# Scattering the experts' results to token order instead of gathering them

## The chip, the cores and the metric

The kernel runs on 1 core of one Trainium2 chip. The metric is the device time of one execution in microseconds (us), as the median of several runs. A profiled execution of the kernel before is there beside the times; PE is TensorE, DVE is VectorE, ACT is ScalarE, POOL is GpSimd and SP is SyncE.

## The reference

Two transformer blocks over 1024 tokens of 1024 channels, in f32. Each block ends in a mixture of experts: every token chooses two experts (16 experts in the first block, 32 in the second), each expert is a gated two-layer network with 256 hidden channels, and the two results of a token are added with their weights. Cut to what matters here:

```
# first block; the second is alike with 32 experts
for e in range(N_EXPERTS):
    he = silu(t @ exp_w1[e]) * (t @ exp_w3[e])
    y = y + comb[:, e:e + 1] * (he @ exp_w2[e])      # comb is zero but for two experts of a token
h = h + y
```

## The kernel before

Attention and the other mixers come first in each block, then the router (`route`), then the experts (`moe`), then a part that adds the results to the stream: `join` behind the first block's experts (it also starts the second block), and the loop at the end of `run` behind the second block's.

**Places.** Each expert has a place, a fixed number of rows: nine of 192 and seven of 128 in the first block (2624 rows), and 128, 128, 128, 192, three more of 128, four of 96, six of 80, ten of 64 and five of 48 in the second (2704 rows). A place of 192 is worked as two units, 128 and 64 rows. There are 1024 x 2 = 2048 choices, so many rows are empty. What does not fit goes to a loop over blocks of 128 rows, `moe_rest`, whose trip count is read from the router's result.

**Experts.** `moe` walks the places in a fixed order. In iteration i, POOL issues an indirect gather of the tokens of the place after next (`gather`, L1702, from the DRAM tensor `vs` by the table `idx`), PE turns the tokens of the next place (`xT`, L1726 or L1715), works `up` of this place (L1748), then `down` of the place before (L200). ACT (and DVE) evacuate that result to a tile y, and POOL writes y to rows of the DRAM tensor `ys` (L1801). So POOL's queue, which is worked in order, holds: gather of place i+2, half of a weight's split (L176), the one or two puts of place i-1, gather of place i+3, and so on. SP issues all weight loads, eight pieces ahead; six pieces make an expert.

**Reading back.** `fetch` gathers, for a tile of 128 tokens, the rows of their first and of their second choice by the table `slot`: two indirect DMAs of 512 KB on POOL (L1894). `join` fetches three tiles ahead. The last loop of `run` fetches six tiles ahead, adds them (L1903) and stores each tile on SP (L2711).

**Zeros.** Rows past the fixed places are written by the loop alone and may never be written, so `make_ys` fills them with zeros: 40 DMAs of 512 KB on SP from a tile that DVE clears (L840, L846), issued while the first block's branches are merged.

Storage is a ring of 42 tiles of 128 x 1056 f32 (`t()`), worked through in program order. Each engine and each queue waits in order; the waits come from the program's tiles and tensors, by the range that an instruction names.

Of the kernel before, what the change touches and what calls it, by code (L numbers as in the profile page):

```python
# [9 lines left out]
F32 = mybir.dt.float32  # L10
# [9 lines left out]
T = 1024  # L20
D = 1024
# [17 lines left out]
class Side:  # L39
    """Work that fills in between the blocks of a main stream, in its own order."""  # L40
# [20 lines left out]
    # a block of the main stream of this length has been put in  # L61
# [31 lines left out]
    # the most blocks that any counts (2 * T in all, the places past NP in falling order) leave to the loop  # L93
# [21 lines left out]
class Kern:  # L115
# [87 lines left out]
    def consts(self):  # L203
# [24 lines left out]
        gp.iota(self.tid, pattern=[[0, 2], [1, 8]], base=0, channel_multiplier=0,  # L228
# [4 lines left out]
        # ones under the high and the low part of each head's row  # L233
# [27 lines left out]
    # 1/sqrt(ss/n + eps), some columns at a time, with one step of Newton's after the table's root  # L261
# [23 lines left out]
    # transpose four token tiles (already scaled), gains on the way, hi and lo  # L285
# [10 lines left out]
    # out^T tile = w^T u^T, three passes, with the columns ahead of the tokens or without  # L296
# [26 lines left out]
    # ======================================================= attention  # L323
    # maxima of half of one head's queries from a first product, fed back as a row
    def attn_max(self, H, half):
# [3 lines left out]
        for ii in range(4):  # L329
# [7 lines left out]
            for j, (c0, c1, s0) in enumerate(ch):  # L337
# [30 lines left out]
    # halves of heads one after the other; the product with v follows LAG blocks behind  # L368
# [60 lines left out]
    # two heads to one tile of channels: unnormalized values and the sums  # L429
# [5 lines left out]
    # halves of pairs of heads one after the other; the products with v follow LAG blocks behind,  # L435
    # those of the two heads next to each other in the array, and so do the sums of the rows
# [78 lines left out]
    # sums of the rows of both heads and halves, each on a quarter of the partitions  # L515
# [9 lines left out]
    # what is left of a pair once its last product is in, with the delays in blocks  # L525
# [16 lines left out]
    # ======================================================= block one  # L542
# [39 lines left out]
    # rows and their norm, channel major; v of the tokens that are ready between the steps  # L582
# [89 lines left out]
    # v with a column of ones for each head, 128 keys to a block, and the forget gates  # L672
# [49 lines left out]
        # to rows [head, token], running sum, negated, as hi and lo  # L722
# [18 lines left out]
    # l = log(1 + w) for w >= 0  # L741
# [13 lines left out]
    # channel-major k and q of two heads  # L755
# [11 lines left out]
    # two sets of operands of the product of q and k, with their constant rows  # L767
# [6 lines left out]
    # rows of sums and partial maxima, filled once where nothing is written later  # L774
# [13 lines left out]
    # 1 / sums: the four rows go over all partitions and back  # L788
# [47 lines left out]
    # rows of the experts' results; those that only the loop may write start as zeros  # L836
    def make_ys(self):
        self.ys = {}
        z = self.t()
        self.ve.memset(z, 0.0)  # L840
        for lay in self.lays:
            ys = self.ys[lay.E] = self.d([lay.RB + lay.MS * 128, D], F32, f"ys{lay.E}")
            for b in range(lay.MS):
                if b % 3 == 0:
                    yield
                self.sy.dma_start(ys[lay.RB + b * 128:lay.RB + (b + 1) * 128, :], z[:, :D])  # L846
# [76 lines left out]
    def pair_units(self, pairs, prep, Hs, done):  # L923
# [5 lines left out]
        # what waits for another engine is put off behind the next steps  # L929
# [48 lines left out]
    # inputs of the convolution and of the pool, channel major, with the keys ahead of the tokens  # L978
# [35 lines left out]
    def conv_one(self):  # L1014
# [13 lines left out]
        # layer norm over the 256 channels, then silu  # L1028
# [78 lines left out]
    def merge_one(self):  # L1107
# [27 lines left out]
        zero = self.make_ys()  # L1135
        for m in range(8):
            next(zero, None)
            next(zero, None)
            g = gate()
            mt = self.t()  # L1140
            branch(self.w(), 0, self.ych, 4, g, True, mt)
            self.gp.dma_start(mc[m], mt[:, :T])
        self.ych = None
        for _ in zero:
            pass
# [28 lines left out]
    # ======================================================= output product, norm, router  # L1174
    # the router's weights ahead of their use
# [10 lines left out]
    # merged channels of half of the tokens, two to a tile  # L1186
# [13 lines left out]
    def mix_out(self, resid, g_ffn, lay, tag):  # L1200
# [9 lines left out]
        # high and low parts of the merged channels  # L1210
# [6 lines left out]
        # on the rows before their norm, with its gains in the weights  # L1217
        # some rows at a time, in three steps
# [31 lines left out]
        # a step of the product for rows i  # L1250
# [38 lines left out]
        def evac(i, p0, p1):  # L1289
# [16 lines left out]
            # columns stored as (k p) with d = p * 8 + k  # L1306
# [68 lines left out]
    # ======================================================= routing  # L1375
    # experts of each token, tiles t0 to t1: one-hot rows of both choices and their running sums
    def choose(self, L, lay, t0, t1, R):
# [24 lines left out]
        # one-hot of the first place that holds the maximum  # L1402
# [29 lines left out]
        # rank of each choice within its expert  # L1432
# [3 lines left out]
        # tokens by expert and rank, by one-hot products  # L1436
# [9 lines left out]
        for k in range(2):  # L1446
            ve.tensor_tensor(C2[:, k, :, 1, :], R["A"][:, k, ts, :], bc(self.tid[:, ts], E), op=OP.mult)
# [8 lines left out]
    def route_new(self, lay):  # L1456
# [15 lines left out]
        # on partitions: the experts twice, the second time with a weight of 128  # L1472
# [7 lines left out]
        # the experts' numbers under their counts, the fixed ones ahead, as a row and as a column  # L1480
# [16 lines left out]
    def route(self, L, lay, R, tag):  # L1497
# [8 lines left out]
        # places of the experts  # L1506
# [13 lines left out]
        te.matmul(ps[:1, 2 * E:3 * E], R["ec"][:E2], perm, start=True, stop=True)  # L1520
        idx = sm.tile([128, 3, E], I32, name="idx", tag="idx", bufs=1)
        ve.tensor_copy(idx[:, 0, :], ps[:, 0:E])
        ve.tensor_copy(idx[0:1, 2, :], ps[0:1, 2 * E:3 * E])
        ve.tensor_copy(idx[:W - 128, 1, :], ps[:W - 128, E:2 * E])
        r = dict(lay=lay, idx=idx)
# [4 lines left out]
    # slots of the choices and their weights, and the loop's blocks  # L1530
    def route_rest(self, L, lay, R, tag, r, tr, ar, bt):
# [63 lines left out]
        slot = sm.tile([128, 16], I32, name="slot", tag="slot", bufs=1)  # L1595
        ve.tensor_copy(slot, sl)
# [3 lines left out]
        # tokens of the loop's blocks  # L1600
# [1143 lines left out]
```

## Time and profile before

| | us |
|---|---|
| median of 3 runs | 2699.92 |
| lowest and highest run | 2695.99, 2700.57 |
| span of the profiled execution | 2697.9 |
| PE busy | 2482.7 (92%) |
| POOL busy | 665.8 (25%) |

The span runs from the first to the last instruction of one profiled execution, whose own time is not given apart from it; the median of the runs is 2.0 us above it. The first block's experts run from about 899 to 1135 us of the span, `join` from about 1143 us, the second block's experts from about 2293 to 2651 us, and the last loop behind them.

### The profile page before, as it was taken

The page shows a single profiled execution, that of the slowest core. Times are in us where ns is not written, and L with a number is a line of the kernel's source. Part 1 is how long each engine was busy: PE and PEld are TensorE (multiplying, and loading weights), DVE is VectorE, ACT ScalarE, POOL GpSimd, SP SyncE. Part 2 cuts the span into 40 slices and gives each one's busy share as a digit, 9 for nine tenths or more (in the row PEclk, how much of TensorE's full clock was granted, in tenths as well). Part 3 has the DMA queues.
Part 4 walks back from the last instruction along what each step waited for, and adds up shares of the span by engine and source line. Part 5 has one row for each costly group of instructions (what it writes and reads, how often), then busy time and mean ns, then how long its engine had stood idle before and what let it go on. Part 6 is the DMA issues. An engine that isn't in the chain of part 4 may idle for free. (4 is left out here: it accounts for less than half of the span.)

```text
span 2697.9 us, 35605 instructions
## 1 busy us (share of the span) xinstructions
PE 2482.7 (92%) x12353; PEld 1919.6 (71%) x12353; DVE 1651.6 (61%) x2653; ACT 1235.6 (46%) x2169; POOL 665.8 (25%) x698
## 2 busy tenths in 40 slices
PE   7999999999999799769999999989999998898992
PEld 7975696778877577668788888986555576665551
DVE  4235339742345798674665463567777465898884
ACT  4236521231132567665334333436555532677771
POOL 1011111000001234450000002244455511343343
PEclk9999999999999899989999999999999999899996
DMA  4000245522252699762222120334222254699996
GB/s 135 25 9 10 62 137 195 199 89 88 94 181 80 205 305 340 246 196 71 63 86 61 57 77 20 112 122 139 75 84 90 92 196 156 214 357 356 353 356 237
DMA packets 251766, 402.78 MB, mean 149 GB/s; under 512 B 31280, under 2 KB 142160, under 8 KB 251584
## 3 DMA queue, kind: packets, MB, share of 16 engines
q1 hardware_dynamic: 221616, 300.25, 34.3%
q0 software_dynamic: 29968, 100.22, 10.7%
q8 instruction: 99, 1.62, 0.2%
q14 instruction: 83, 0.68, 0.1%
HBM read 304.71 MB, written 95.29 MB: 148 GB/s over the span
## 5 line engine op out<-in xcount | busy, mean ns | idle before, releaser
L200 PE MATMUL ps<-s,s 128*128 128x512 f32 (+14 forms) x8804 | 1911.0, 376 | 32.4 <-ACT s L196 6.0
L200 PEld LDWEIGHTS ps<-s,s 128*128 128x128 f32 (+6 forms) x8804 | 1510.0, 186 | 398.3 <-issue 67.9
L178 DVE TENSOR_TENSOR s<-s,s 128x1024 fp32r<-128x1024 f32 (+4 forms) x373 | 499.5, 1358 | 408.0 <-ACT s L174 404.2
L174 ACT ACTIVATE s<-s 128x1024 fp32r<-128x1024 f32 (+3 forms) x423 | 418.8, 1038 | 79.3 <-DMA s<-in_w_up 24.5
L1748 PE MATMUL ps<-s,s 128*128 128x512 f32 (+4 forms) x1320 | 328.1, 404 | 4.3 <-DVE s L178 3.4
L1748 PEld LDWEIGHTS ps<-s,s 128*128 128x128 f32 (+4 forms) x1320 | 217.7, 169 | 92.5 <-DVE s L178 7.4
L176 POOL TENSOR_TENSOR s<-s,s 128x1024 fp32r<-128x1024 f32 x50 | 137.3, 2747 | 111.6 <-ACT s L174 99.5
L350 DVE TENSOR_REDUCE mx<-ps 128x1 f32<-128x512 f32 (+10 forms) x304 | 142.5, 506 | 17.1 <-PE ps L200 15.4
L484 ACT ACTIVATE s<-ps 128x512 f32<-128x512 f32 (+1 forms) x192 | 93.9, 489 | 113.2 <-PE ps L200 109.6
L1130 ACT ACTIVATE s<-ps 128x512 f32<-128x512 f32 x24 | 14.4, 598 | 247.4 <-PE ps L200 237.6
L499 POOL TENSOR_TENSOR s<-s,s 128x512 f32<-128x512 f32 (+1 forms) x64 | 108.4, 1693 | 47.6 <-ACT s L486 22.4
L1801 POOL DMA_DIRECT2D ys<-s x58 | 33.5, 578 | 229.7 <-ACT s L1800 184.9
L446 PE MATMUL ps<-s,s 128*64 128x512 f32 (+3 forms) x384 | 84.8, 523 | 0.8 <-DVE mx L350 0.8
L1023 DVE SCALAR_TENSOR_TENSOR s<-s,c,s 128x1024 f32<-128x1024 f32 x60 | 82.7, 1379 | 1.5
L1726 PE MATMUL ps<-c,s 128*128 128x128 f32 (+4 forms) x392 | 46.5, 264 | 38.3 <-DMA s<-vs,idx 38.2
L1726 PEld LDWEIGHTS ps<-c,s 128*128 128x128 f32 (+4 forms) x392 | 39.9, 147 | 52.8 <-issue 24.1
L414 ACT ACTIVATE s<-ps 128x512 f32<-128x512 f32 (+4 forms) x112 | 49.4, 447 | 48.8 <-PE ps L200 47.6
L1702 POOL DMA_INDIRECT s<-vs,idx x58 | 63.1, 1088 | 32.1 <-issue 17.3
L196 ACT ACTIVATE s<-s 128x512 fp32r<-128x512 f32 (+2 forms) x49 | 36.7, 775 | 74.1 <-DVE s L2190 35.3
L197 DVE TENSOR_TENSOR s<-s,s 128x512 fp32r<-128x512 f32 (+2 forms) x49 | 41.7, 884 | 44.0 <-ACT s L196 44.0
L283 ACT ACTIVATE s<-s 128x1024 f32<-128x1024 f32 (+1 forms) x25 | 26.4, 1055 | 89.3 <-issue 43.5
L1729 DVE TENSOR_TENSOR s<-ps,s 128x512 fp32r<-128x512 f32 (+3 forms) x82 | 49.5, 633 | 25.4 <-ACT s L1728 24.3
(473 smaller groups left out, 2293.8 us busy)
## 6 DMA issues: line engine op xcount, KB each, us to landing
s<-in_w_in SPq DMA_DIRECT2D x80, 512.0 KB
s<-in_exp_w SPq DMA_DIRECT2D x128, 256.0 KB
s<-in_w_gate SPq DMA_DIRECT2D x128, 256.0 KB
s<-in_w_up SPq DMA_DIRECT2D x128, 256.0 KB
s<-in_w_down SPq DMA_DIRECT2D x64, 512.0 KB
ys<-s SPq DMA_DIRECT2D x40, 512.0 KB
s<-in_exp_w SPq DMA_DIRECT2D x32, 512.0 KB
ys<-s POOLq DMA_DIRECT2D x23, 512.0 KB, 6.9
```

What stands on the lines that cost most here:

```text
L174: self.ac.activation(hi[:, :n], st[:, :n], AF.Copy)
L176: self.gp.tensor_tensor(lo[:, :n], st[:, :n], hi[:, :n], op=OP.subtract)
L178: self.ve.tensor_sub(lo[:, :n], st[:, :n], hi[:, :n])
L200: self.te.matmul(out, lhsT, rhs, start=start, stop=stop)
L350: self.ve.tensor_reduce(mx[:, ii, j:j + 1], ps[:, c0 - s0:c1 - s0], axis=AX.X, op=OP.max)
L446: self.te.matmul(o[64 * hh:64 * hh + 64, c:], H["v"](j)[:rows], pf[:rows, hh, c:], start=first, stop=last and not c, skip_group_check=True)
L484: self.ac.activation(pf[:rows, hh, c:], s[:rows, c:], AF.Exp)
L499: eng.tensor_tensor(acc[:rows, :, c:], acc[:rows, :, c:], pf[:rows, :, c:], op=OP.add)
L1023: ve.scalar_tensor_tensor(a[:, :T], gl[:, k:k + T], cw[:, c, k:k + 1], a[:, :T], op0=OP.mult, op1=OP.add)
L1702: gp.indirect_dma_start(out=x[:n, :D], out_offset=None, in_=vs, in_offset=bass.IndirectOffsetOnAxis(ap=r["idx"][:n, j, b:b + 1], axis=0))
L1726: te.transpose(ps[:, (k - q) * n:(k - q + 1) * n], x[:, k * 128:(k + 1) * 128], idn)
L1748: te.matmul(ps[:m].rearrange("p (w h) -> p w h", w=2), x, rhs, start=c == 0 and j == 0, stop=c == 7 and j == len(ops) - 1)
```

## The change

The expert's result goes straight to the row of its token and choice: `ys` gets 2 x 1024 rows (row 1024 k + token for choice k), and each unit's put is an indirect scatter by a new table `dst`. Empty rows get the index 2048, which is past the bound and is skipped. `fetch` is then two plain loads of 128 rows on SP. Nothing has to be zero beforehand, `slot` is gone, and the last loop of `run` fetches all eight tiles ahead. The table of tokens is the new table's low ten bits.

```
-        gp.iota(self.tid, pattern=[[0, 2], [1, 8]], base=0, channel_multiplier=0,
+        gp.iota(self.tid, pattern=[[1, 16]], base=-16, channel_multiplier=0,
...
-        z = self.t()
-        self.ve.memset(z, 0.0)
-        for lay in self.lays:
-            ys = self.ys[lay.E] = self.d([lay.RB + lay.MS * 128, D], F32, f"ys{lay.E}")
-            for b in range(lay.MS):
-                if b % 3 == 0:
-                    yield
-                self.sy.dma_start(ys[lay.RB + b * 128:lay.RB + (b + 1) * 128, :], z[:, :D])
+        self.ys = {lay.E: self.d([2 * T, D], F32, f"ys{lay.E}") for lay in self.lays}
...
-        ve.tensor_copy(idx[:, 0, :], ps[:, 0:E])
+        dst = sm.tile([128, 2, E], I32, name="dst", tag="dst", bufs=1)
+        ve.tensor_scalar(dst[:, 0, :], ps[:, 0:E], 2048.0, None, op0=OP.add)
+        ve.tensor_scalar(idx[:, 0, :], dst[:, 0, :], 1023, None, op0=OP.bitwise_and)
         ve.tensor_copy(idx[0:1, 2, :], ps[0:1, 2 * E:3 * E])
-        ve.tensor_copy(idx[:W - 128, 1, :], ps[:W - 128, E:2 * E])
+        ve.tensor_scalar(dst[:W - 128, 1, :], ps[:W - 128, E:2 * E], 2048.0, None, op0=OP.add)
+        ve.tensor_scalar(idx[:W - 128, 1, :], dst[:W - 128, 1, :], 1023, None, op0=OP.bitwise_and)
...
+    def put(self, ys, ix, y):
+        self.gp.indirect_dma_start(out=ys, out_offset=bass.IndirectOffsetOnAxis(ap=ix, axis=0), in_=y,
+                                   in_offset=None, bounds_check=2 * T - 1, oob_is_err=False)
...
-                gp.dma_start(ys[s:s + n, :], y[:n, :D])
+                self.put(ys, r["dst"][:n, s, b:b + 1], y[:n, :D])
...
-            self.sy.dma_start(ys[bass.ds(i * 128 + lay.RB, 128), :], y[:, :D])
+            self.put(ys, ix[:, 1:2], y[:, :D])
...
-            self.gp.indirect_dma_start(out=y[:, :D], out_offset=None, in_=ys,
-                                       in_offset=bass.IndirectOffsetOnAxis(
-                                           ap=r["slot"][:, 8 * k + i:8 * k + i + 1], axis=0))
+            self.sy.dma_start(y[:, :D], ys[k * T + i * 128:k * T + i * 128 + 128, :])
...
-        F = {i: self.fetch(i, b2["r"], ys) for i in range(6)}
+        F = {i: self.fetch(i, b2["r"], ys) for i in range(8)}
         for i in range(8):
             h = self.combine(i, b2["r"], F.pop(i))
             self.sy.dma_start(self.out[0][i * 128:(i + 1) * 128, :], h[:, :D])
-            if i + 6 < 8:
-                F[i + 6] = self.fetch(i + 6, b2["r"], ys)
```

The loop's table of tokens (`lix`) gets a second column with the target rows in the same way.

## Rows read from the trace of the kernel before

**Rows 1.** Busy time by engine in one stretch of the first experts; then PE clock, DMA share, GB/s.
```profile
1040.00:1080.00 40.00, 38.95 (x196) 31.57 (x195) 34.33 (x38) 31.61 (x49) 15.08 (x12) 1.00 1.00 354
```
**Rows 2.** The same for one stretch of the second experts.
```profile
2590.00:2620.00 30.00, 27.29 (x137) 15.01 (x136) 24.25 (x25) 23.51 (x34) 11.96 (x9) 1.00 1.04 357
```
**Rows 3.** What the loop's own write of ys (L1887) left in the trace.
```profile
nothing on L1887; most used: ['L200', 'L1748', 'L1683', 'L178', 'L1726', 'L446', 'L174', 'L2618', 'L1235', 'L167', 'L350', 'L484', 'L1227', 'L1768', 'L414', 'L1840', 'L1715', 'L1702', 'L521', 'L2050', 'L176', 'L1681', 'L349', 'L486', 'L357'
```
**Rows 4.** POOL in order of time around a place of two units: start us, us, instruction.
```profile
1053.59 0.60 POOL L1801 DMA_DIRECT2D ys<-s  x1 [3.43 <-ACT s L1800]
1056.21 0.58 POOL L1801 DMA_DIRECT2D ys<-s  x1 [2.02 <-DVE s L1798]
1057.10 0.99 POOL L1702 DMA_INDIRECT s<-vs,idx  x1 [0.30 <-issue]
1058.40 1.08 POOL L1702 DMA_INDIRECT s<-vs,idx  x1 [0.30 <-issue]
```
**Rows 5.** PE in order of time: where the tokens of that gather are turned.
```profile
1067.16 1.03 PE L1726 MATMUL ps<-c,s 128*128 128x128 f32 x8
```
**Rows 6.** The puts of the first experts by line, and their time to landing.
```profile
L1801 POOL DMA_DIRECT2D ys<-s x25: 537/591/603, 939.9 to 1135.0; - x25
...
DMA to landing us min/median/max: 2.9/6.6/8.1
```
**Rows 7.** The gathers of the first experts by line, their time to landing.
```profile
DMA to landing us min/median/max: 4.8/8.0/9.1
```
**Rows 8.** POOL in order of time, one iteration of the second experts.
```profile
2599.01 0.58 POOL L1801 DMA_DIRECT2D ys<-s  x1 [3.06 <-ACT s L1800]
2599.89 0.91 POOL L1702 DMA_INDIRECT s<-vs,idx  x1 [0.31 <-DVE s L178]
...
2609.91 0.58 POOL L1801 DMA_DIRECT2D ys<-s  x1 [4.71 <-ACT s L1800]
```
**Rows 9.** PE's longest wait in the second experts: us in total, times, longest us.
```profile
PE ps L1726 <- DMA s<-vs,idx: 31.5, 21, 7.2
```
**Rows 10.** All engines in order of time, end of the first experts and start of join.
```profile
1131.30 1.12 POOL L1801 DMA_DIRECT2D ys<-s  x2
...
1135.00 0.59 POOL L1801 DMA_DIRECT2D ys<-s  x1 [2.58 <-ACTq L1840]
...
1143.08 1.00 POOL L1894 DMA_INDIRECT s<-ys,slot  x1 [7.49 <-issue]
...
1144.43 2.36 DVE L178 TENSOR_TENSOR s<-s,s 128x1024 fp32r<-128x1024 f32 x2 [12.96 <-ACT s L174]
...
1149.74 1.28 DVE L1984 SCALAR_TENSOR_TENSOR s<-s,cw,s 128x1024 f32<-128x1024 f32 x1 [0.96 <-DMA s<-ys,slot]
...
1159.57 3.68 PE L2050 MATMUL ps<-c,s 128*128 128x128 f32 x16 [25.76 <-DVE s L2047]
```
**Rows 11.** All engines in order of time, the end of the kernel.
```profile
2651.34 0.53 POOL L1801 DMA_DIRECT2D ys<-s  x1 [3.55 <-ACTq L1840]
...
2658.53 1.00 POOL L1894 DMA_INDIRECT s<-ys,slot  x1 [6.66 <-issue]
...
2692.73 1.28 DVE L1903 SCALAR_TENSOR_TENSOR s<-s,cw,s 128x1024 f32<-128x1024 f32 x1 [0.95 <-DMA s<-ys,slot]
```
**Rows 12.** The loop's branches (L1840) on SP and POOL: first and last start us.
```profile
L1840 SPq COMPARE_BRANCH  x6: 33/38/57, 1117.2 to 2656.8; - x6
...
L1840 POOLq COMPARE_BRANCH  x6: 33/38/54, 1135.1 to 2657.6; - x6
```
**Rows 13.** Busy time by engine in two stretches of the end; columns as in rows 1.
```profile
2665.00:2670.00 5.00, 0.00 (x0) 0.00 (x0) 4.28 (x4) 0.00 (x0) 4.08 (x4) 0.50 0.96 337
...
2675.00:2680.00 5.00, 0.00 (x0) 0.00 (x0) 3.73 (x4) 0.00 (x0) 3.90 (x4) 0.50 1.03 420
```
**Rows 14.** The router's last step before the first gather, by line, one for each block.
```profile
L1524 DVE CAST idx<-ps x2: 152/160/169, 898.8 to 2290.9; 64x16 int32<-64x16 f32 x1, 64x32 int32<-64x32 f32 x1
```
**Rows 15.** PE's longest wait between 420 and 460 us, where the zeros are cleared and written.
```profile
PE ps L1096 <- DVE s L1088: 5.1, 1, 5.1
```

More of the change, by code (lines that the diff above doesn't have):

```diff
@@ L837, in make_ys @@
     def make_ys(self):
-        self.ys = {}
-        z = self.t()
-        self.ve.memset(z, 0.0)
-        for lay in self.lays:
-            ys = self.ys[lay.E] = self.d([lay.RB + lay.MS * 128, D], F32, f"ys{lay.E}")
-            for b in range(lay.MS):
-                if b % 3 == 0:
-                    yield
-                self.sy.dma_start(ys[lay.RB + b * 128:lay.RB + (b + 1) * 128, :], z[:, :D])
+        self.ys = {lay.E: self.d([2 * T, D], F32, f"ys{lay.E}") for lay in self.lays}
     def attn_one(self):
@@ L1134, in merge_one @@
         mc = self.d([8, 128, T], F32, "mc1")
-        zero = self.make_ys()
+        self.make_ys()
         for m in range(8):
-            next(zero, None)
-            next(zero, None)
             g = gate()
@@ L1143, in merge_one @@
         self.ych = None
-        for _ in zero:
-            pass
         for m in range(8):
@@ L1446, in choose @@
         for k in range(2):
-            ve.tensor_tensor(C2[:, k, :, 1, :], R["A"][:, k, ts, :], bc(self.tid[:, ts], E), op=OP.mult)
+            ve.tensor_tensor(C2[:, k, :, 1, :], R["A"][:, k, ts, :], bc(self.tid[:, 8 * k + t0:8 * k + t1], E), op=OP.mult)
             ve.tensor_tensor(R1[:, k], self.io[:, None, :W].to_broadcast([128, n, W]),
@@ L1521, in route @@
         idx = sm.tile([128, 3, E], I32, name="idx", tag="idx", bufs=1)
-        ve.tensor_copy(idx[:, 0, :], ps[:, 0:E])
+        dst = sm.tile([128, 2, E], I32, name="dst", tag="dst", bufs=1)
+        ve.tensor_scalar(dst[:, 0, :], ps[:, 0:E], 2048.0, None, op0=OP.add)
+        ve.tensor_scalar(idx[:, 0, :], dst[:, 0, :], 1023, None, op0=OP.bitwise_and)
         ve.tensor_copy(idx[0:1, 2, :], ps[0:1, 2 * E:3 * E])
-        ve.tensor_copy(idx[:W - 128, 1, :], ps[:W - 128, E:2 * E])
-        r = dict(lay=lay, idx=idx)
+        ve.tensor_scalar(dst[:W - 128, 1, :], ps[:W - 128, E:2 * E], 2048.0, None, op0=OP.add)
+        ve.tensor_scalar(idx[:W - 128, 1, :], dst[:W - 128, 1, :], 1023, None, op0=OP.bitwise_and)
+        r = dict(lay=lay, idx=idx, dst=dst)
         R["ix"] = None
@@ L1594, in route_rest @@
         ve.tensor_add(sl, sl, cap)
-        slot = sm.tile([128, 16], I32, name="slot", tag="slot", bufs=1)
-        ve.tensor_copy(slot, sl)
         nr = sm.tile([128, 1], I32, name="nr", tag="nr", bufs=1)
@@ L1627, in route_rest @@
         ve.scalar_tensor_tensor(ixf, ps[:, MS:2 * MS], 128.0, ixf, op0=OP.mult, op1=OP.add)
-        lix = sm.tile([128, MS], I32, name="lix", tag="lix", bufs=1)
-        ve.tensor_copy(lix, ixf)
+        lix = sm.tile([128, MS, 2], I32, name="lix", tag="lix", bufs=1)
+        ve.tensor_scalar(lix[:, :, 1], ixf, 2048.0, None, op0=OP.add)
+        ve.tensor_scalar(lix[:, :, 0], lix[:, :, 1], 1023, None, op0=OP.bitwise_and)
         ps = None
@@ L1663, in route_rest @@
         ve.tensor_copy(wi, wf)
-        r.update(slot=slot, nr=nr, lix=lix, cw=cw, wi=wi)
+        r.update(nr=nr, lix=lix, cw=cw, wi=wi)
     def plan_moe(self, w1, w3, w2, lay, box):
@@ L1703, in gather @@
                                       in_offset=bass.IndirectOffsetOnAxis(ap=r["idx"][:n, j, b:b + 1], axis=0))
-                XG[b].append((x[:n], self.idn[:n, :n], s, n))
+                XG[b].append((x[:n], self.idn[:n, :n], j, n))
         def xT(b):
@@ L1840, in moe_rest @@
         with self.tc.For_i(0, n, 1) as i:
-            ix, wx = self.s(1, I32, tag="lx", bufs=1), self.s(6, I32, tag="lw", bufs=1)
-            ve.tensor_copy(ix, r["lix"][:, bass.ds(i, 1)])
+            ix, wx = self.s(2, I32, tag="lx", bufs=1), self.s(6, I32, tag="lw", bufs=1)
+            ve.tensor_copy(ix, r["lix"][:, bass.ds(i, 1), :].rearrange("p o c -> p (o c)"))
             ve.tensor_copy(wx, r["wi"][:, bass.ds(i, 1), :].rearrange("p o c -> p (o c)"))
```

## The prediction

> **What bounds the kernel now.** I read the page's busy times first, then the granted clock and busy times by stretch, then the queues in order of time around each place where the change acts, since no average says what ends last there. Four places matter. In the first experts PE has the least room: it is busy 38.95 of 40 us, and the DMA engines are full too (share 1.00) [rows 1]. In the second experts PE is busy 27.29 of 30 us while the DMA share is 1.04 at 357 GB/s [rows 2], so the transfers pace that stage; still PE's longest wait there is for the token gathers, 31.5 us in 21 waits [rows 9], so how early POOL issues a gather counts as well. In `join` PE stands still for 25.76 us until the first two tiles are added [rows 10]. At the end there is nothing but reading back, adding and storing: 2697.9 - 2658.53 = 39.4 us from the first gather [rows 11].
>
> **The change part by part.** The sum is made against the span of 2697.9 us; the median of the runs, 2699.92 us, is 2.0 us above it, so the sum is added to the median.
>
> *Router.* Two DVE instructions are added in each block ahead of the first gather, each like the last cast of 0.16 us [rows 14]; with a gap of some 0.04 us that is 0.4 us a block at most, and 0.2 if the first gather waits for its own half alone. I take +0.7 for both. The removed `slot` cast and the changed `lix` steps lie under the experts' matmuls.
>
> *Zeros.* A DVE clear and 40 writes (20 MB) go. Nearly all of it is under PE's work. The exception: between 420 and 460 us PE waits 5.1 us for a DVE line [rows 15], and the clear is queued on DVE ahead of it. Bounds 0 and the whole wait of 5.1; I take -1, about the time of one DVE pass over a tile (1.28 us [rows 11]).
>
> *The put itself.* No row shows a scatter. The nearest below is the direct put, 0.58 us, above it the gather, 0.91 to 1.08 [rows 4, 8]. I take the gather, as it also works from a table: +0.4 us for each put, with twice the gather's time as the far end, since the bounds check has no row.
>
> *Order of the puts.* This decides. Before, each put names its own rows, and nothing keeps the second unit of a place behind the first: the puts at 1053.59 and 1056.21 are 2.62 us apart [rows 4], though a put takes 6.6 us (2.9 to 8.1) to land [rows 6]. After, every put names the whole of `ys` as its target, so by the program any two overlap, and I expect each to wait on POOL until the one before has landed. For places of one unit this costs nothing: the put before was an iteration ago (10.9 us in the second experts [rows 8]). For places of two units it does. The first put starts at 1053.59 and lands 6.6 + 0.4 later, at 1060.6; the second starts then, not at 1056.21, and the gather queued behind it on POOL starts at 1060.6 + 0.95 + 0.3 = 1061.85, not at 1057.10. It lands 8.0 us later [rows 7], at 1069.85, and PE wants those tokens at 1067.16 [rows 5]: a stall of 2.7 us. With the shortest landings (2.9 and 4.8) the gather lands at 1063 and there is no stall; with the longest (8.1 and 9.1) it is 5.3 us. As a stall also thins the DMA traffic and so shortens the landings, I take 2.0. Seven places of 192 rows have a gather behind them, so +14 (0 to 37). In the second experts only one place has two units, ahead of the stretch that I count; nothing is added.
>
> The Trainium skill bears on this: its page "DMA: Bandwidth & Descriptors", section "Two DMAs through the same engine are not ordered", says that only the completion semaphore orders two transfers, and that the issuing engine must wait for it before the dependent one; the queue gives no order. So the overlap cannot be had for free by sharing POOL's queue: by that rule the wait stands and the sum is the one below; no row here shows two overlapping writes, so the trace neither agrees nor differs.
>
> *The end of the first experts.* The last puts start at 1131.30 (two) and 1135.00, where traffic is thin and landing takes the shortest time, 2.9 us [rows 6, 10]. Chained they start at 1131.30, 1134.6 and 1137.9: 2.9 later, with the dearer put 3.3. Against that `join` gains: its first addition has both rows at 1149.74, while DVE is free from 1146.79 and the first addition takes 1.28; plain loads that land early enough would let the second start at 1148.1, so at most -1.6 [rows 10]. Together +1.7.
>
> *Bytes.* The loop never ran [rows 3], so all 2048 choices sit in places, and 576 and 656 rows of 4 KB are no longer written. In the first experts PE has the say, so 0. In the second, places 7 to 31, which hold 1744 of 2704 rows, run with the DMA full; their share of 656 is 423 rows, 1.73 MB, at 357 GB/s 4.9 us [rows 2]. The dearer put delays each gather by 0.4 us and PE does wait for gathers [rows 9], so I take -3; bounds -7.5 (all 656 rows) and the loss in rival D.
>
> *The end.* SP passes the loop's branch at 2656.8, POOL at 2657.6 and starts its gather at 2658.53, 0.9 later [rows 11, 12]. SP's first load would start near 2656.8 + 0.9 + 0.4 = 2658.1, 0.4 earlier. What moves is the same: sixteen loads and eight stores of 512 KB, 12.58 MB. While POOL gathers and stores mix, the stretch moves 337 GB/s, later 420 [rows 13]. All of it at 420 is 30.0 us; with 1.5 for the first bytes and the last store's tail (2697.9 - 2692.73 - 1.28 = 3.9 less 1.25 of transfer) it is 34.1 instead of 39.4. So -5.6; if only the engines' idle share (0.96 against 1.03 over the first 15 us) comes back, -1 to -2. I take -5.
>
> The row at 337 GB/s, against 420 in the same mix later, says that something beyond the engines' rate was lost while POOL issued; I go by that row, and the other reading is rival E.
>
> **Sum.** 0.7 - 1 + 14 + 1.7 - 3 - 5 = +7.4 us: 2699.9 + 7.4 = 2707.3 us, rounded to 2707.
>
> **Rivals.**
> - *B, ordered but covered.* Landings in the first experts turn out short. From a put that lands in 4.5 us and a gather in 7, the second unit's gather lands at 1053.59 + 4.9 + 1.25 + 7 = 1066.7, before PE's 1067.16, and the stalls go. At 0.5 us each the sum is 7.4 - 14 + 3.5 = -3.1: 2697. For it: landings reach down to 2.9. Against: the medians.
> - *C, the puts are not ordered.* Then the chained terms go (14 and 3.3): 7.4 - 17.3 = -9.9: 2690. For it: the puts before ran 2.62 us apart unhindered. Against: they named separate rows. This is the case on the other side, and it decides as soon as a second unit's put starts within 3 us of the first.
> - *D, the second experts lose on POOL.* An iteration there is put, gather, landing, turn: 2599.01 to 2609.91 is 10.9 us, of which put to gather is 0.88 [rows 8]. If that chain and not the bytes sets the pace, +0.4 us for 31 experts is +12 in place of -3, and with a put above 1.3 us more: 2722. Against: the DMA share of 1.04.
> - *E, the end keeps its pace.* The loads then move at the mean rate of before, whoever issues them, and the end gives only the start 0.4 us earlier and about one issue of 1.0 us on POOL, -1.5 in place of -5: 7.4 + 3.5 = 10.9, 2711. For it: the engines' share was 0.96 already at 337 GB/s [rows 13]. Against: the share rose by 0.07, the rate by a quarter. The Trainium skill has this as a rule ("DMA: Bandwidth & Descriptors", section "Issuing engines are not separate DMA queues"): the same 16 engines move the data whoever issues, and only the sequencer's issue time is saved. The trace so far leaves it open.
>
> **How the numbers follow.** Chances: the forecast 0.45, B 0.20, C 0.18, E 0.10, D 0.07. A measurement of this kernel can tell about 0.2%, 5.4 us. The forecast's own spread (0 to 5.3 us a stall) crosses that bound: of its 0.45 I give 0.27 to slower, 0.12 to the same, 0.06 to faster; B 0.11 same, 0.09 faster; C 0.13 faster, 0.03 same, 0.02 slower (if its puts are dear); E 0.09 slower, 0.01 same; D slower. Together slower 0.45, the same 0.27, faster 0.28. The range 2688 to 2719 takes in C with some room and stalls of up to 3.6 us each; D and the longest landings lie above it, C with the full byte saving lies below it. The forecast's own range is 2698 to 2719.
>
> **What would show it.** In the trace after: the gap between a place's two scatters (7 us by the forecast, under 3 by C); PE's wait for token gathers in the first experts (about 14 us more); the scatter's time on POOL (0.95); the DMA rate behind the last loop (420 from the start) and 34 us from the first load to the end; PE's idle time in `join`. The prediction is wrong if the scatters of one place overlap, or if POOL spends well over 1 us on one.

## The result and the profile after

The changed kernel takes 2730.37 us (median of 4 runs, 2726.21 to 2733.31) against 2700.24 for the kernel before beside it (2695.99 to 2703.85): ratio 1.0109, 95% interval 1.0095 to 1.0122. It is 1.1% slower; forecast was 2707, and the range ended at 2719.

The spans of the profiled executions are 2724.4 and 2697.9 us, 26.5 apart. The profiled execution of the kernel after is its fastest run (2726.21 us), so the parts below account for 26.5 of the 30.1 us between the medians. To see where they lie, I divide both at the same five events: POOL's first token gather, PE's last product of the first experts, the first product of `join`, POOL's first gather of the second experts, PE's last product there. First the rows of the timeline of the kernel after at which the parts meet (start us, us, instruction; in brackets the idle time before and what ended it):

```profile
899.68 1.08 POOL L1698 DMA_INDIRECT s<-vs,idx  x1 [6.30 <-DVE idx L1516]
...
1158.01 3.04 PE L200 MATMUL ps<-s,s 128*128 128x512 f32 x12 [1.13 <-ACT s L1770]
1188.18 2.18 PE L2044 MATMUL ps<-c,s 128*128 128x128 f32 x9 [27.14 <-DVE s L2041]
...
2679.53 2.99 PE L200 MATMUL ps<-s,s 128*48 128x512 f32 x12 [0.81 <-ACT s L1770]
```

PE stands idle for 27.14 us before 1188.18, so its first experts end at 1161.04; the second experts' first gather is at 2321.69, and PE ends at 2682.52. The kernel before, divided in the same way, has 899.10, 1133.81, 1159.57 [rows 10], 2293.38 and 2650.11. In us:

| part | before | after | difference |
|---|---|---|---|
| to the first gather | 899.1 | 899.7 | +0.6 |
| first experts | 234.7 | 261.4 | +26.7 |
| to join's first product (PE idle) | 25.8 | 27.1 | +1.4 |
| to the second experts' first gather | 1133.8 | 1133.5 | -0.3 |
| second experts | 356.7 | 360.8 | +4.1 |
| end | 47.8 | 41.9 | -5.9 |

Nearly all of the loss lies in the first experts; the second experts' +4.1 is taken up below. The first experts' busy time by engine, over the whole part, before and then after (columns as in [rows 1]: the stretch, its length, PE, PEld, DVE, ACT and POOL busy with counts, PE clock, DMA share, GB/s):

```profile
899.10:1133.80 234.70, 220.90 (x1067) 177.37 (x1067) 192.37 (x258) 165.93 (x252) 93.51 (x69) 0.96 0.87 288
```

```profile
899.68:1161.04 261.36, 232.67 (x1067) 185.82 (x1067) 188.53 (x258) 167.56 (x252) 101.35 (x68) 0.91 0.77 250
```

PE does the same 1067 products. It is idle for 28.7 us instead of 13.8 (+14.9), and it is busy for 11.8 us longer over the same products, while its mean granted clock falls from 0.96 to 0.91. The two make the 26.7. The DMA share falls as well, 0.87 to 0.77: over the stage the transfers had more room than before, not less.

One place shows how it comes about. POOL in order of time around the same place of two units as in [rows 4]:

```profile
1061.91 1.09 POOL L1684 DMA_INDIRECT ys<-s,dst  x1 [2.34 <-ACT s L1796]
1071.00 0.91 POOL L1684 DMA_INDIRECT ys<-s,dst  x1 [8.00 <-DMA ys<-s,dst]
1072.23 0.97 POOL L1698 DMA_INDIRECT s<-vs,idx  x1 [0.31 <-issue]
```

The scatters of one place start 9.09 us apart, where the puts before were 2.62 apart [rows 4], and the second waits for a DMA to `ys`. The gather behind the second scatter, at 1072.23, brings the tokens that PE needs next. In order of time PE has nothing left to do at 1075.64 and stands still for 5.00 us (before, it turned these tokens without a wait, [rows 5]):

```profile
1072.70 2.94 PE L200 MATMUL ps<-s,s 128*128 128x512 f32 x12
1080.64 1.94 PE L1722 MATMUL ps<-c,s 128*128 128x128 f32 x8 [5.00 <-DMA s<-vs,idx]
...
1085.35 6.96 PE L1744 MATMUL ps<-s,s 128*128 128x512 f32 x19
```

Eight turns of tokens take 1.94 us here and took 1.03 [rows 5]. Windows of 5 us around this stall show the granted clock (columns as above):

```profile
1075.00:1080.00 5.00, 0.65 (x3) 0.19 (x1) 4.39 (x3) 2.64 (x4) 3.89 (x2) 1.00 0.88 250
1080.00:1085.00 5.00, 3.63 (x19) 2.84 (x19) 1.38 (x2) 1.76 (x3) 1.24 (x2) 0.52 1.03 308
1085.00:1090.00 5.00, 5.00 (x14) 3.92 (x14) 4.03 (x6) 4.48 (x7) 1.34 (x1) 0.50 0.75 280
1090.00:1095.00 5.00, 5.00 (x22) 4.03 (x22) 3.00 (x3) 1.49 (x3) 1.37 (x1) 0.96 0.57 193
```

The granted clock is at its lower level (0.50, 1.2 GHz) for nearly 10 us behind the stall; a full-time busy PE gets 14 products done in 5 us, and 22 once the clock is back. PE's waits for gathered tokens in the first experts, in total us, times and longest, before and then after:

```profile
PE ps L1726 <- DMA s<-vs,idx: 6.7, 3, 5.3
PE ps L1715 <- DMA s<-vs,idx: 1.5, 2, 1.1
```

```profile
PE ps L1722 <- DMA s<-vs,idx: 23.8, 6, 6.9
PE ps L1711 <- DMA s<-vs,idx: 3.1, 3, 1.7
```

They grew by 18.7 us in all. Three stalls, of 6.94, 5.00 and 4.39 us, make 16.3 of it, and each has a slow stretch behind it. The other two, with windows behind them:

```profile
1034.39 1.94 PE L1722 MATMUL ps<-c,s 128*128 128x128 f32 x8 [6.94 <-DMA s<-vs,idx]
...
1115.67 1.94 PE L1722 MATMUL ps<-c,s 128*128 128x128 f32 x8 [4.39 <-DMA s<-vs,idx]
```

```profile
1035.00:1040.00 5.00, 5.00 (x19) 4.28 (x18) 3.50 (x5) 4.24 (x6) 0.02 (x1) 0.58 0.24 96
...
1115.00:1120.00 5.00, 3.67 (x19) 2.88 (x20) 1.38 (x2) 1.79 (x3) 1.61 (x2) 0.50 1.04 318
1120.00:1125.00 5.00, 5.00 (x14) 3.93 (x15) 4.07 (x6) 4.45 (x6) 1.39 (x1) 0.54 0.71 272
```

From each of these three turns to a later turn of tokens at full clock, PE is busy for 27.99, 16.59 and 16.23 us (windows from 1034.39 to 1062.38, 1080.64 to 1097.96 and 1115.67 to 1132.56). The same work took 25.71, 12.54 and 12.55 us before (1027.28 to 1054.04, 1067.16 to 1079.70 and 1092.83 to 1105.38). So 10.0 of the 11.8 us of longer work lie behind the three stalls.

The longest stall stands at a place that left less time. In the kernel before, POOL and PE there:

```profile
1016.22 0.60 POOL L1801 DMA_DIRECT2D ys<-s  x1 [8.14 <-ACT s L1800]
...
1027.28 1.04 PE L1726 MATMUL ps<-c,s 128*128 128x128 f32 x8
```

From the place's first put to the turn of the tokens gathered behind its second it is 11.1 us, against 13.6 at the place of [rows 4, 5].

The end, from SP's first load, and its windows (columns as above), against [rows 11, 13]:

```profile
2683.73 0.88 POOL L1684 DMA_INDIRECT ys<-s,dst  x1 [3.23 <-ACTq L1836]
2689.28 13.89 SPq L1890 DMA_DIRECT2D s<-ys  x16
...
2712.20 2.61 DVE L1897 SCALAR_TENSOR_TENSOR s<-s,cw,s 128x1024 f32<-128x1024 f32 x2 [0.29 <-DMA s<-ys]
```

```profile
2693.00:2698.00 5.00, 0.00 (x0) 0.00 (x0) 4.00 (x4) 0.00 (x0) 0.00 (x0) 0.50 1.01 380
2698.00:2703.00 5.00, 0.00 (x0) 0.00 (x0) 4.90 (x5) 0.00 (x0) 0.00 (x0) 0.50 1.03 417
2703.00:2708.00 5.00, 0.00 (x0) 0.00 (x0) 4.95 (x4) 0.00 (x0) 0.00 (x0) 0.50 1.03 412
```

From the first load to the end it is 35.1 us (39.4 before, 34.1 forecast), and the rate is 380 to 417 GB/s as soon as data flow, where 337 stood before [rows 13].

### The profile page after: what moved, and what is told of

Its sections match the earlier page's. It is cut to its first block, busy times and chain, and to the rows that moved or that the text cites. A ratio compares the mean times of both kernels' runs of the same rounds, so it can differ in the third digit from the quotient of the medians.

```text
span 2724.4 us, 35633 instructions
## 1 busy us (share of the span) xinstructions
PE 2497.4 (92%) x12353; PEld 1932.6 (71%) x12353; DVE 1649.4 (61%) x2656; ACT 1237.5 (45%) x2169; POOL 656.3 (24%) x666
## 5 line engine op out<-in xcount | busy, mean ns | idle before, releaser
L178 DVE TENSOR_TENSOR s<-s,s 128x1024 fp32r<-128x1024 f32 (+4 forms) x373 | 490.0, 1334 | 408.1 <-ACT s L174 405.8
L1744 PE MATMUL ps<-s,s 128*128 128x512 f32 (+4 forms) x1320 | 335.3, 411 | 1.3 <-DVE s L178 1.3
L1744 PEld LDWEIGHTS ps<-s,s 128*128 128x128 f32 (+4 forms) x1320 | 224.9, 174 | 89.5 <-DVE s L178 3.2
L176 POOL TENSOR_TENSOR s<-s,s 128x1024 fp32r<-128x1024 f32 x50 | 132.7, 2656 | 98.7 <-ACT s L174 84.1
L1684 POOL DMA_INDIRECT ys<-s,dst x58 | 68.9, 1188 | 249.8 <-ACT s L1796 149.1
L197 DVE TENSOR_TENSOR s<-s,s 128x512 fp32r<-128x512 f32 (+2 forms) x49 | 41.8, 886 | 44.7 <-ACT s L196 44.7
L1724 ACT ACTIVATE s<-ps 128x512 fp32r<-128x512 f32 (+3 forms) x82 | 42.6, 556 | 52.8 <-PE ps L1722 52.5
```

Source lines behind the costliest of these rows:

```text
L176: self.gp.tensor_tensor(lo[:, :n], st[:, :n], hi[:, :n], op=OP.subtract)
L178: self.ve.tensor_sub(lo[:, :n], st[:, :n], hi[:, :n])
L1684: self.gp.indirect_dma_start(out=ys, out_offset=bass.IndirectOffsetOnAxis(ap=ix, axis=0), in_=y, in_offset=None, bounds_check=2 * T - 1, o ...
L1744: te.matmul(ps[:m].rearrange("p (w h) -> p w h", w=2), x, rhs, start=c == 0 and j == 0, stop=c == 7 and j == len(ops) - 1)
```

## The experiments

Eleven more kernels. Their parts, divided as above, from one profile of each, and their ratios to the kernel before, measured beside each:

| kernel | first experts | PE idle to join | second experts | end | median us | ratio (95%) |
|---|---|---|---|---|---|---|
| before | 234.7 | 25.8 | 356.7 | 47.8 | 2700 | |
| after | 261.4 | 27.1 | 360.8 | 41.9 | 2730 | 1.0109 (1.0095 to 1.0122) |
| gather first | 246.6 | 26.8 | 358.5 | 41.2 | 2709 | 1.0038 (1.0022 to 1.0054) |
| before, gather first | 232.5 | 26.1 | 360.3 | 47.6 | 2698 | 0.9991 (0.9982 to 1.0000) |
| two targets | 232.2 | 23.9 | 360.0 | 41.8 | 2712 | 1.0038 (1.0021 to 1.0054) |
| wait alone | 255.0 | 26.4 | 360.0 | 48.0 | 2725 | 1.0096 (1.0081 to 1.0111) |
| plain loads | 235.6 | 23.8 | | | 2723 | 1.0072 (1.0057 to 1.0087) |
| no skip | 264.8 | 28.0 | 362.5 | 43.0 | 2729 | 1.0099 (1.0081 to 1.0117) |
| deferred | 235.5 | 27.1 | 360.8 | 41.7 | 2702 | 0.9995 (0.9985 to 1.0006) |
| deferred, gather first | 245.9 | 27.1 | 359.8 | 40.8 | 2713 | 1.0041 (1.0028 to 1.0055) |
| second block only | 237.7 | 25.7 | 360.4 | 40.8 | 2698 | 0.9991 (0.9979 to 1.0002) |
| end plain | 236.0 | 26.6 | 358.4 | 41.5 | 2697 | 0.9984 (0.9973 to 0.9994) |
| six ahead | 261.0 | 27.1 | 362.2 | 41.9 | 2728 | 1.0099 (1.0083 to 1.0115) |

The first experts of "second block only" and of "end plain" put and gather as before: 237.7 and 236.0 against 234.7 us. So one profile of that part can differ by 3 us from another. The texts before the runs of "gather first" to "deferred, gather first" count the first experts to POOL's last put (235.9 us before, 266.5 after); the table and the last three texts count to PE's last product.

**Is it the wait between the scatters?** Three kernels: the gather moved ahead of the scatters in the kernel after, the same move in the kernel before, and the second units scattered to a tensor of their own.

```
 gather first (after and before)
+        for b in O[:3]:
+            gather(b)
...
-            if i + 2 < len(O):
-                gather(O[i + 2])
...
             WK[b] = [self.w() for _ in range(2)]
+            if i + 3 < len(O):
+                gather(O[i + 3])
             if i:
                 down(O[i - 1])

 two targets (after; the 32 writes of zeros to ys are left out here)
...
-                self.put(ys, r["dst"][:n, s, b:b + 1], y[:n, :D])
+                self.put(self.yo[lay.E] if s else ys, r["dst"][:n, s, b:b + 1], y[:n, :D])
```

> The changed kernel with the gather of the place after next put into POOL's queue ahead of the two scatters instead of behind them. Queue theory (the second scatter of a place waits on POOL for the first, and the token gather queued behind it comes late): the first experts go back from 267 us to about 236, the total to 2692 to 2702. Late-buffer rival (the results' tiles come free late, so SP's weight loads start late): the wait of the second scatter and SP's wait for it (37 us) stay, and with them most of the 31 us: 2720 or more. Dear-scatter rival (the scatter costs too much by itself, on POOL or in landing): at least half of the 31 us stays.

> The kernel before with the same move of the gather. Queue theory: nothing waits there between two puts, so the first experts keep their 236 us; in the second experts PE's wait for gathers (31.5 us) shrinks if the put ahead of the gather sets it: 2690 to 2700. If the transfers alone pace that stage: 2698 to 2701.

> The changed kernel with the second units' results scattered to a tensor of their own that nothing reads (those rows are left out of the sum; the tokens' rows are zeroed beforehand by 32 stores of 512 KB), so that the two scatters of a place do not name the same tensor. Queue theory and late-buffer rival: the second scatter no longer waits, the first experts go back to 236 to 242 us, the total to 2698 to 2706. Dear-scatter rival: they stay at 255 or more, total 2718 or more.

With two targets nothing orders the pair, and the first experts are back at 232.2 us: dear scatters alone cost nothing that shows there. POOL in order of time, the same place in this kernel, and the whole part:

```profile
1069.47 1.12 POOL L1690 DMA_INDIRECT ys<-s,dst  x1 [2.30 <-ACT s L1802]
1072.33 0.91 POOL L1690 DMA_INDIRECT yo<-s,dst  x1 [1.73 <-DVE s L1800]
```

```profile
917.86:1150.04 232.18, 218.45 (x1067) 175.31 (x1067) 187.77 (x258) 165.81 (x252) 105.38 (x69) 0.98 0.85 282
```

Its total, 2711.70 us, misses the 2698 to 2706 that I expected, because its first gather starts at 917.86 instead of 899.68. The 32 writes of zeros go out in one burst from 384.9 to 422.5 us, and DVE waits 17.6 us for them there (L1120).

With the gather first PE no longer waits for tokens (6.5 us in one wait, that of the first place), but only 14.8 of the 26.7 us return, and 2709.49 us lies between what I expected and the late-buffer rival's 2720. Counted to the last put, half of the loss stays (251.3 us), so the kernel with two targets is needed to exclude the dear scatter. The second scatter still stands behind the first (7.05 to 12.95 us, but for the last pair), and now POOL's half of a weight's split (L176) stands behind it. In that kernel POOL, then PE, in order of time:

```profile
1033.47 4.64 POOL L1684 DMA_INDIRECT ys<-s,dst  x1 [0.30 <-issue]
1046.42 1.32 POOL L1684 DMA_INDIRECT ys<-s,dst  x1 [8.30 <-DMA s<-in_exp_w]
1047.74 2.58 POOL L176 TENSOR_TENSOR s<-s,s 128x1024 fp32r<-128x1024 f32 x1
```

```profile
1046.99 2.81 PE L1744 MATMUL ps<-s,s 128*128 128x512 f32 x11 [0.26 <-DVE s L178]
1054.35 0.80 PE L1744 MATMUL ps<-s,s 128*128 128x512 f32 x1 [4.54 <-ACT s L174]
```

PE has its tokens and lacks split weights. In the kernel before, the move takes 2.2 us off the first experts in one pair of profiles, less than such profiles differ by, and nothing that can be told off the total: 2698.05 us fits both of the ranges named.

**The wait without the scatter.** The kernel before with its direct puts, the second unit written one row early, so that it overlaps the first and must wait.

```
...
-                gp.dma_start(ys[s:s + n, :], y[:n, :D])
+                o = s - (s > lay.base[b])
+                gp.dma_start(ys[o:o + n, :], y[:n, :D])
```

> The kernel before, direct puts and gathered reads, with the second unit of a place of 192 written one row too early, so that it overlaps the first by one row and has to wait for it (one row of a unit is lost by it, the last row of the place is zeroed beforehand). Queue theory: the wait alone makes the first experts 20 to 31 us longer, total 2718 to 2731. Dear-scatter rival: there is no scatter, so 2698 to 2705.

POOL and the whole stage in this kernel:

```profile
1060.88 0.60 POOL L1805 DMA_DIRECT2D ys<-s  x1 [5.23 <-ACT s L1803]
1068.44 0.58 POOL L1805 DMA_DIRECT2D ys<-s  x1 [6.97 <-DMA ys<-s]
1069.33 0.99 POOL L1705 DMA_INDIRECT s<-vs,idx  x1 [0.31 <-PE ps L1751]
```

```profile
899.30:1154.26 254.96, 229.50 (x1067) 182.65 (x1067) 188.63 (x258) 167.28 (x252) 88.18 (x68) 0.93 0.81 265
```

With no scatter at all 20.3 of the 26.7 us are there: 11.7 idle and 8.6 of slower products (clock 0.93), and 2725.02 us is in the range that I expected. The other 6.4 I put down to what scatters add to the chain, which no run shows by itself: here the second put follows after 7.56 us, with scatters after 9.09.

**What must not stand behind the wait.** The kernel after with the second unit's scatter issued in the next place's `up`, behind the gathers; then both moves together.

```
+        second = []
+
+        def flush():
+            while second:
+                self.put(ys, *second.pop(0))
...
                 wh, wl = self.w()
                 next(gen, None)
+                if kk == 1:
+                    flush()
...
-                self.put(ys, r["dst"][:n, s, b:b + 1], y[:n, :D])
+                a = r["dst"][:n, s, b:b + 1], y[:n, :D]
+                if s:
+                    second.append(a)
+                else:
+                    self.put(ys, *a)
...
```

> The after kernel, but the second unit's scatter is issued later: not right behind the first one, but in the next place's up, behind the gather, when the first scatter has landed. My theory, the wait in POOL's queue: the gather no longer stands behind a wait, the first experts come back to 234 to 242 us from 266.5, and the time to 2697 to 2706. Rival, the tile: the second unit's tile of the ring is freed as late as before, so weight loads on SP still wait for the scatter and the first experts stay at 250 or more, the time at 2712 or more.

> The deferred second scatter and, as well, the gather put ahead of the scatters in POOL's queue. My theory: first experts 234 to 240 us, join and end as in the after kernel, 2692 to 2700 us: level with the kernel before or a little faster. Rival as in the run before (the tile freed late): 250 us or more for the first experts, 2710 or more in all.

Deferred, the first experts take 235.5 us: the loss is gone, and the total, 2701.68 us, is as I expected and level with the kernel before. The whole part, and POOL at one place, where the wait is still there:

```profile
901.23:1136.72 235.49, 222.51 (x1067) 178.67 (x1067) 186.39 (x258) 166.15 (x252) 101.39 (x68) 0.96 0.84 278
```

```profile
1056.35 1.13 POOL L1684 DMA_INDIRECT ys<-s,dst  x1 [2.29 <-DMA s<-in_exp_w]
1057.79 0.96 POOL L1703 DMA_INDIRECT s<-vs,idx  x1 [0.30 <-issue]
1059.05 0.91 POOL L1703 DMA_INDIRECT s<-vs,idx  x1 [0.30 <-issue]
1065.90 0.93 POOL L1684 DMA_INDIRECT ys<-s,dst  x1 [5.95 <-DMA ys<-s,dst]
```

POOL idles 5.95 us for the landing, with the gathers already issued. The late tile, my rival, costs nothing that shows: SP still waits 27.4 us in all for scatters to land (37.3 in the kernel after).

With both moves it is worse again, 245.9 us (251.0 to the last put, where I had expected at most 240), and 2713.17 us in all. Both figures lie in the rival's ranges, but not for its reason: SP waits only 5.9 us for scatters in this kernel. POOL there:

```profile
1031.04 1.78 POOL L1703 DMA_INDIRECT s<-vs,idx  x1 [0.16 <-issue]
1033.12 0.91 POOL L1703 DMA_INDIRECT s<-vs,idx  x1 [0.30 <-PE ps L1771]
1034.33 1.01 POOL L1684 DMA_INDIRECT ys<-s,dst  x1 [0.30 <-issue]
1044.81 0.93 POOL L1684 DMA_INDIRECT ys<-s,dst  x1 [9.47 <-PE ps L200]
1045.74 2.77 POOL L176 TENSOR_TENSOR s<-s,s 128x1024 fp32r<-128x1024 f32 x1
```

The first scatter now goes out behind two gathers, the second follows only 10.5 us later, and the split behind it is late. The longest such gap is 11.74 us here and 9.55 with the second scatter deferred alone. That the gathers' transfers hold up the scatter's landing is how I read it; it wasn't tried by itself.

**Which edit gives the join and the end?**

```
 plain loads (before); end plain: in the last loop alone; both fetch eight tiles ahead at the end
-            self.gp.indirect_dma_start(out=y[:, :D], out_offset=None, in_=ys, ...)
+            self.sy.dma_start(y[:, :D], ys[k * T + i * 128:k * T + i * 128 + 128, :])

 six ahead (after)
-        F = {i: self.fetch(i, b2["r"], ys) for i in range(8)}
+        F = {i: self.fetch(i, b2["r"], ys) for i in range(6)}
...
+            if i + 6 < 8:
+                F[i + 6] = self.fetch(i + 6, b2["r"], ys)
```

> Leaves the rows' order out: the kernel before, its puts and its queue untouched, but the tokens read back by plain loads on SP, of rows of places instead of the rows of their choices, so the sums are of other rows; all eight tiles are fetched ahead at the end. My theory: the join and the end of the after kernel owe their gain to the plain loads alone. The join's part gives back about 2.8 us (23.3 us between the last put and the first gather of the second experts becomes about 20.5), the end 5.9 (46.6 from the last put to the end becomes about 41), first and second experts keep 236 and 358: span and time 8 to 9 us shorter, ratio 0.9968, 2691 to 2694 us. Rival: the end's gain belongs to the direct rows (nothing written past the tokens' rows, shorter traffic before it); then the end stays above 44 us and the time within 3 us of before.

> The kernel before in all but its last part: the end reads rows of places by plain loads on SP, all eight tiles ahead, so the last sums are of other rows; join still gathers, and all before the end is untouched. My theory: the end's gain belongs to the loads alone: 41 to 43 us behind PE's last product instead of 47.8, time 2692 to 2695. Rival, that the gain needs the scattered rows: 46 us or more, no change in the time. The second experts here run the instructions of before a further time: 356 to 358 us speaks for a real loss of 4 us in the after kernel, 359 to 361 says that executions differ by that much.

> The after kernel, but the last loop fetches six tiles ahead as in the kernel before, the other two behind stores on SP. Which of the two edits at the end gives the 5.9 us? My theory, who issues: the end stays at 41 to 43 us behind PE's last product. Rival, how far ahead: 44 us or more. Else as after: 261 us in the first experts, 359 to 362 in the second, 2727 to 2734 in all.

The first of these was badly chosen: with other sums going on, the loop behind the second experts ran (its gathers, L1837, stand in the trace behind 2654 us), which I put down to tokens that chose other experts. So its second half and its total, 2722.65 us against the expected 2691 to 2694, say nothing. Its join does: PE is idle for 23.83 us there, 1.9 less than before. With the plain loads confined to the end, the end takes 41.5 us and the time is 2697.23 us (0.9984, 0.9973 to 0.9994): not the 2692 to 2695 that I expected, but the end's own gain is all there, without a scatter. Its second experts, 358.4 us, fall between the two ranges that I had named for them and decide nothing. With six tiles ahead the end stays at 41.9 and the total at 2728.49, as expected. So it is the plain loads on SP, not the depth and not the scattered rows. Whether the queue or the plain form of the load does it isn't separated: no kernel issues plain loads on POOL. In all kernels whose end loads on SP it takes 40.8 to 43.0 us, in all that gather on POOL 47.6 to 48.0.

**Do the saved bytes pace the second experts?** The kernel after, with the empty rows written too, to one extra row.

```
-        self.ys = {lay.E: self.d([2 * T, D], F32, f"ys{lay.E}") for lay in self.lays}
+        self.ys = {lay.E: self.d([2 * T + 1, D], F32, f"ys{lay.E}") for lay in self.lays}
...
-                                   in_offset=None, bounds_check=2 * T - 1, oob_is_err=False)
+                                   in_offset=None, bounds_check=2 * T, oob_is_err=False)
```

> The after kernel, but empty rows are written as well, all of them to one extra row behind the tokens' rows (ys has 2049 rows, and the bound is 2048), so the bytes saved by skipping are written again. Theory that bytes pace the second experts: they grow by some 5 us over the after kernel's 362 (1.7 MB at 357 GB/s), the first experts stay or grow by the longer landings (266 to 280), in all 2733 to 2745. Rival: the saved bytes pace nothing, and the second experts lose on POOL's dearer puts: 360 to 364 us again, in all 2727 to 2733. If many writes to one row are dear by themselves, landings grow far beyond 6.5 us and both are off.

2728.93 us, inside the rival's 2727 to 2733, and 362.5 us for the second experts, 1.7 above the kernel after and within what profiles differ by. The bytes were moved: 314 GB/s over that part against 308, some 2.7 MB more. The skipped bytes pace nothing that can be seen.

**The good half alone.** Places, zeros and gathers for the first block as before; scatters and plain loads for the second.

```
...
-                self.put(ys, r["dst"][:n, s, b:b + 1], y[:n, :D])
+                if lay.E == 16:
+                    o = lay.base[b] + 128 * s
+                    gp.dma_start(ys[o:o + n, :], y[:n, :D])
+                else:
+                    self.put(ys, r["dst"][:n, s, b:b + 1], y[:n, :D])
...
```

> The change in the second block alone: the first block's experts write places and join gathers them, as before, and the second block's experts scatter and the end reads plainly, as after. Counted from the end of PE's last product of each stage, the kernel before spends 234.7 us in the first experts, 25.8 to the first product of join, 356.7 in the second experts and 47.8 behind them; after, 41.9 behind them. My theory: the first three parts stay, and the end's 5.9 us are kept, so 2692 to 2694 us, ratio 0.997 to 0.998. Rival: the scatters cost the second experts the 4 us by which they were longer in the after kernel; then they take 360 to 362 and the time is 2696 to 2699.

The end is at 40.8, but the first experts, unchanged, came out 3.0 us longer in this profile and the second 3.7; 2697.97 us misses my 2692 to 2694 and lies in the rival's 2696 to 2699, as do the 360.4 us of the second experts. It is a gain of 0.1% that the interval (0.9979 to 1.0002) does not tell from none. Only "end plain" has an interval clear of 1, by 0.16% in the middle, and it reads the rows of places and so adds other rows than it should. No version that gives the right sums beats the kernel before by an amount that these runs can tell.

## Why the prediction was wrong

The direction, the place and the mechanism were right; the size of the term that decides was not.

- **Order of the puts: the step that failed.** Forecast +14, from a gap of 7 us and seven stalls of 2.0, each priced at its length; measured +26.7. The wait is there at every place of two units, with gaps of 6.3 to 9.1 us in the thick of the stage; rivals B and C fall. Three things made the term too small.
  - The gap was 9.09 us at the place that the prediction read, so the stall was 5.00 us there and not 2.7. The step from 2.7 down to 2.0, for landings that a stall would shorten, went the wrong way.
  - That one place stood for all seven. At the place with the longest stall PE wanted the tokens 2.5 us sooner after the first put. PE's waits for tokens grew by 18.7 us (forecast about 14), 16.3 of them in three stalls of 4.4 to 6.9 us. That the idle time grew by 14.9 us in all, near the forecast 14, is luck: other waits shrank.
  - No term priced the clock. Behind each long stall the granted clock lies at 0.50, and over the stage the same products cost 11.8 us more. The prediction read the clock by stretch, but put the cost of a stall beyond its length at nothing, without a reason. Its own rows held a sign: sixteen turns take 3.68 us behind PE's idle 25.76 us [rows 10], 0.23 us each, and eight take 1.03 us in full work [rows 5], 0.13 each; the granted clock from 1159 to 1165 us of the kernel before is 0.51.

  The Trainium skill describes it ("TensorE: Matmul & The Clock Gate", section "HAM oscillation — how this bites in real kernels"): PE waiting on transfers between bursts of products gets its clock cut back, and the next burst starts slow. The trace agrees, 0.50 to 0.52 behind the 5.00 us stall. The 20.3 us of the wait alone, and the return to 232.2 and 235.5 us when the pair isn't ordered or the gathers don't stand behind the wait, leave no other cause of that size. The term's own bounds, 0 to 37, held the 26.7; the range, which allowed 3.6 us a stall, did not.
- **The put itself.** 0.95 us forecast; 1.01 in the first experts and 1.08 in the second, by the median. Right.
- **The end of the first experts and join.** +1.7 forecast as +3.3 and -1.6; PE's idle time grew by 1.4. The plain loads alone take off 1.9 (23.8 us, and 23.9 with two targets, where the pair isn't ordered either), which leaves 3.3 for the chained last puts (1158.74, 1162.91, 1166.13). Right, both halves.
- **Router and zeros.** +0.7 and -1; the first gather is 0.6 later, and the middle 0.3 shorter. In the other kernels that gather starts between 898.3 and 901.2 (917.9 with two targets), so neither term is resolved. The -1 rested on PE's wait of 5.1 us [rows 15]; without the clear that wait is 5.1 us again (L1088, for DVE's L1080), so the clear did not set it: it ran at 384.23 us for 0.94, ahead of the stretch that [rows 15] names, with DVE idle behind it.
- **Bytes.** -3 forecast, +4.1 in the pair of profiles. Writing the bytes again costs 1.7 in another pair, so no saving can be seen: I read the limit from a stretch of 30 us with a DMA share of 1.04 [rows 2], but over the whole stage it was 0.93 before and 0.92 after. Whether scatters cost something there stays open. Direct puts with the gather behind them took 356.7, 360.0 and 358.4 us, scatters 360.8, 360.0, 360.8, 360.4 and 362.2 (362.5 with all rows): 2.5 apart in the mean and touching at 360.0. Rival D's 12 us is excluded.
- **The end.** -5 forecast, -5.9 measured; rival E (-1.5) falls. The sum was right, its halves less so: the first load starts 1.7 us sooner behind PE's last product (6.76 us against 8.42; forecast 0.4), and from there to the end it is 4.3 us shorter (forecast 5.3). The Trainium skill's rule on issuers ("DMA: Bandwidth & Descriptors", section "Issuing engines are not separate DMA queues") allows only the issue time as the gain. That can be squared with the rows if the issue is counted fully: POOL's sixteen gathers started over 21.6 us (2658.53 to 2680.11), SP's sixteen loads went out in 13.89. Rival E counted one issue of 1.0 us.

In sum: 0.6 + 26.7 + 1.4 - 0.3 + 4.1 - 5.9 = 26.6 us against a forecast of 7.4; 12.7 of the 19.2 between them are the stalls' term, 7.1 the bytes, where profiles of the same instructions differ by 3.3.

## What to carry to other kernels

When several transfers come to name one whole tensor as their target, as here, each waits on its queue for the landing before it; look at what stands behind the wait, and move that ahead or the second transfer back (here the second transfer back, for 26 us, with the wait itself still there; the gathers ahead gave 14.8, since the next thing in the queue then stood behind the wait). Price a stall of PE not by its length alone: see in the windows behind an existing stall what the clock does, and add the slow products. Look at every place for how much time it leaves, not at one. And take a limit from the whole stage, not from its fullest window.

## What was not expected of the hardware

- The three long stalls of PE, of 6.94, 5.00 and 4.39 us, had 2.3, 4.1 and 3.7 us of longer work at the lower clock behind them: 10.0 us beside 16.3, and not more behind the longest. Behind the shorter waits of 0.38 and 0.86 us in the same stage (turns at 953.87 and 998.52) the granted clock stayed at 1.00; behind one of 1.71 us (970.11) it lay at 0.50 from 971 to 974 us.
- Sixteen reads of 512 KB at the end ran at 380 to 417 GB/s from 3.7 us behind the first of them when SP issued them plainly; while POOL gathered them the rate was 337, then 297, then 420 in windows of 5 us from 2665 to 2680 us. The end takes 40.8 to 43.0 us in all kernels of the one kind, 47.6 to 48.0 in those of the other.
- With the token gathers issued ahead of the scatters, the second scatter of a place started as much as 11.74 us behind the first (9.55 with the scatter deferred alone), and 10.4 of the 25.9 us that deferring had gained were lost (245.9 against 235.5 us).
